# Turning the tokens of the first norm into columns: TensorE transposes replaced by VectorE block transposes and transfers through DRAM

## The chip, the cores and the metric

The kernel runs on one core of a Trainium2 chip. A core has TensorE (PE, matmuls; its weight loads are listed as PEld), VectorE (DVE), ScalarE (ACT), GpSimd (POOL) and SyncE (SP, which here only issues transfers). Each engine executes its own instructions in order. Data lies in SBUF (128 partitions), matmul results in PSUM, inputs and scratch in DRAM; transfers between DRAM and SBUF are issued on the queues of SP, ACT or POOL. The metric is the device time of one execution in microseconds, as the median of several runs.

## The reference, cut to what matters

One decoder layer on 1024 tokens of width 1024, in float32:

```python
z = h @ w_in                      # -> pooling group | q | k | v
mix = concat(pool_mixer(..), sliding_window_attention(..)) @ w_out
h = layer_norm(DEEPNORM_ALPHA * h + mix, ln1_g, ln1_b)     # the first norm
ff = square(relu(h @ w_ff1)) @ w_ff2                       # 1024 -> 4096 -> 1024
h = layer_norm(DEEPNORM_ALPHA * h + ff, ln2_g, ln2_b)
gate = sigmoid(h @ w_ple_gate + b_ple_gate)
h = h + gate * (p @ w_ple)
```

The first norm works on rows: a token lies on one partition and its 1024 features lie along it. `h @ w_ff1` needs the same numbers as columns: a feature on each partition and the tokens along it. Between the two the 1024 x 1024 matrix has to be transposed. This is what the change is about.

## The kernel before

**Tiles.** Tokens go in eight tiles `n` of 128. Every fp32 matrix is kept as a high part and a low part (`high`, L101, a cast on ACT; `low`, L106, a subtraction on DVE), and every product of two matrices is three matmuls (`mm3`, L116 to L118): high times high, high times low, low times high.

**Stages.** The layer runs in this order: input projection, attention and pooling (to about 208 us); the output projection, in which `out_left(0)`, `out_right(0..3)` finish tokens 0 to 511 and `out_left(1)`, `out_right(4..7)` finish tokens 512 to 1023; the first norm; the first half of the feed-forward; its second half; the second norm and the gate.

**The first norm.** `norm1(n)` (L544) does five things. `layer_norm` (L405) normalises the row tile `hn[n]` in place: two statistics and two full-width passes on DVE (L408, L424, L121), one pass on ACT (L423), one small power on POOL (L417). `transposed` (L444) then turns the tile on TensorE: eight transposes of 128 x 128 into two PSUM tiles, four into one of the two `pt` buffers (`tr_ps`), four into the single `av` buffer (`tr_av`). ACT scales the row tile and stores it to DRAM scratch `h_dram` for the second norm (L549, L550). Last, the columns are split from PSUM into high and low parts in SBUF (`split_to`, L538). For n below 4 these go to the operands `X["11"]` and `X["21"]`, and for n below 3 a plain copy of the first half goes to `pre`. For n of 4 and above the feed-forward's seven-product scheme (Strassen's kind) wants sums of blocks: `r12`, `t1`, `t2` are formed on ACT and DVE, and the splits go to `X["22"]`, `T1`, `T2` and `T3`. `last_sum` (L574) later forms `T4`.

**The feed-forward's first half.** `early(p)` (L598) for p = 0 to 7 multiplies weight block pairs with `X["11"]` and, in `rest`, with `X["21"]`: 24 matmuls per p in PSUM tiles `mm`. Then a list `order` of products with `T2`, `T3`, `T1`, `22`, `T4` follows, 12 matmuls each, in PSUM tiles `f`; each product's weights are split by `w_split` four products ahead (`AHEAD`).

**Where the order comes from.** The program text gives each instruction a place; the framework's planner then simulates a timeline from its own estimates of durations and writes a fixed order for each engine, taking an instruction of later text first if it is ready first. Buffers come from rings under a tag: `temp` (tag `t`, 6 buffers of 128 x 512), `part` (tag `ws`, 6 of 128 x 1024), `nat` (tag `n`, 8 of 128 x 1024), `wt` (tag `w`, 2). Waits for buffers and data are semaphores that the framework adds. In the text before, `norm1(0..3)` stand behind `out_left(1)`, and `norm1(4..7)` stand ahead of `early(1)`, `early(3)`, `early(5)` and `early(7)`.

**A turn without TensorE** exists already for the second norm: `flip` (L427). DVE transposes blocks of 32 x 32 of a whole 128 x 1024 tile (L429), one transfer stores the result to DRAM scratch `t_dram` (L430), and four transfers bring it back, each filling 32 partitions with pieces from all partitions (L432). All five transfers are on POOL's queue.

Of the kernel before, what the change touches and what calls it, by code (L numbers as in the profile page):

```python
# [61 lines left out]
NPRE = 8  # L62
NSUM = 3
PLAIN = 4
HALVES = (slice(0, HALF), slice(HALF, D))
NLAST = NPAIR - 4
AHEAD = 4
# [3 lines left out]
def layer(ctx, tc, xT, x, pT, w_in, w_pool, pscale, sinks, w_out, ln1, w1, w2, ln2, w_ple, w_gate, bgate, bias, rcount, out):  # L71
# [7 lines left out]
    def nm(s):  # L79
        uid[0] += 1  # L80
        return f"{s}_{uid[0]}"
# [23 lines left out]
    def low(eng, dst, src, hi):  # L105
        return eng.tensor_tensor(out=dst, in0=src, in1=hi.bitcast(F32), op=ALU.subtract)  # L106
# [67 lines left out]
    def tr_ps():  # L174
        return ps.tile([P, 4, P], F32, tag="pt", bufs=2, name=nm("pt"))
# [259 lines left out]
            )  # L435
        return t.rearrange("p (R k c) -> p R k c", R=4, k=NK)

    def tr_av():
        return ps.tile([P, 4, P], F32, tag="av", bufs=1, name=nm("av"))

    def transposed(y, j, pt):
        for k in range(4):
            kt = 4 * j + k
            nc.tensor.transpose(pt[:, k, :], y[:, kt * P : (kt + 1) * P], ident)  # L444
        return pt
# [86 lines left out]

    X = {}

    def block(name, i, c):
        return X[name][:, i, :, c * P : (c + 1) * P].bitcast(F32)

    def split_to(name, c, src, eng):  # L538
        cs = slice(c * P, (c + 1) * P)
        dh = X[name][:, 0, :, cs]  # L540
        high(dh, src)
        return low(eng, X[name][:, 1, :, cs], src, dh)

    def norm1(n):  # L544
        t, c = n // 4, n % 4
        layer_norm(hn[n], gb1)
        a = transposed(hn[n], 0, tr_ps())
        b = transposed(hn[n], 1, tr_av())
        nc.scalar.mul(out=hn[n], in_=hn[n], mul=ALPHA)  # L549
        nc.scalar.dma_start(out=h_dram[n], in_=hn[n])  # L550
        if t == 0:
            if c < 3:
                nc.scalar.copy(out=pre[:, 4 + c].rearrange("p (k t) -> p k t", k=4), in_=a)
            split_to("11", c, a, nc.vector)
            split_to("21", c, b, nc.vector)
        else:
            r12, t1, t2 = temp((P, 4, P)), temp((P, 4, P)), nat([P, 4, P])
            nc.scalar.copy(out=r12, in_=a)
            if c < 3:
                add(t1, a, pre[:, 4 + c].rearrange("p (k t) -> p k t", k=4), ALU.subtract)  # L560
# [594 lines left out]
```

## Time and profile before

| | |
|---|---|
| median of 3 runs | 984.06 us (984.02 to 984.25) |
| the profiled execution's own time | 984.01 us |
| its span in the trace | 982.2 us |
| TensorE busy | 973.8 us, 99% of the span |
| VectorE busy | 750.4 us, 76% |
| ScalarE busy | 470.6 us, 48% |
| GpSimd busy | 129.5 us, 13% |
| moved by transfers | 172.13 MB |

The span is what the trace covers; 1.8 us of the execution's time lie around it. Matmuls are pipelined, so a matmul of 0.39 us can follow another after 0.23 us, and "busy" counts the overlap once. A row of a timeline gives the start, the duration, the engine, the line, the operation and the tiles, and in brackets the idle time before it with what ended it.

### The profile page before, as it was taken

How to read it: one execution, taken by the hardware profiler on the slowest of the kernel's cores; microseconds unless marked ns; L12 is line 12 of the kernel's file. 1: busy time of each engine (PE TensorE's matmuls, PEld its weight loads, DVE VectorE, ACT ScalarE, POOL GpSimd, SP SyncE). 2: the span in 40 equal slices, each digit the busy share in tenths (PEclk: the TensorE clock that was granted, in tenths of full speed). 3: DMA queues.
4: the chain of work that ended last, by engine and by line, in shares of the span. 5: the costliest groups of instructions: out<-in, count | busy, mean ns of one | idle time of the engine just before them, and what ended most of it. 6: DMA issues, size and time to landing. Idle time of an engine off the chain costs nothing.

```text
span 982.2 us, 12301 instructions
## 1 busy us (share of the span) xinstructions
PE 973.8 (99%) x4474; PEld 809.3 (82%) x4474; DVE 750.4 (76%) x1188; ACT 470.6 (48%) x749; POOL 129.5 (13%) x185
## 2 busy tenths in 40 slices
PE   9999999999999999999999999999999999999998
PEld 7888887888888888888888888888888888878887
DVE  5798888895868876867547666888657699799895
ACT  5676666543475443434444344443434354554341
POOL 0013552020010000110000000100011111203210
PEclk9999999999999999999999999999999999999999
DMA  6512142623152544896264794675788866762741
GB/s 220 183 65 86 44 150 75 219 82 115 69 198 103 197 150 159 298 324 242 78 245 172 278 322 149 150 243 194 207 217 190 223 158 225 252 193 77 257 148 55
DMA packets 48188, 172.13 MB, mean 175 GB/s; under 512 B 6016, under 2 KB 7168, under 8 KB 45312
## 3 DMA queue, kind: packets, MB, share of 16 engines
q1 hardware_dynamic: 35584, 130.05, 38.6%
q0 software_dynamic: 10960, 36.71, 14.6%
q10 hardware_dynamic: 1584, 4.59, 1.2%
q8 instruction: 35, 0.57, 0.2%
q14 instruction: 25, 0.20, 0.1%
HBM read 138.82 MB, written 32.51 MB: 174 GB/s over the span
## 4 chain that ended last, share of the span: by engine, by line
PE 94%; DVE 2%; DMA 2%; issue 1%; ACT 1%; DVEq 0%
PE f L117 21%; PE f L118 21%; PE f L116 21%; PE mm L116 8%; PE mm L118 8%; PE mm L117 8%; DMA ws<-in_w_gate 2%; PE pt L322 1%; PE s L299 1%; PE s L298 1%; PE av L328 1%; PE av L327 1%; DVE w L106 0%; PE s L116 0%; ACT c L101 0%
## 5 line engine op out<-in xcount | busy, mean ns | idle before, releaser
L117 PE MATMUL f<-x,w 128*128 128x512 f32 x448 | 174.0, 389 | 0.4 <-DVE x L106 0.4
L118 PE MATMUL f<-x,w 128*128 128x512 f32 x448 | 173.9, 389 | 0.0
L116 PE MATMUL f<-c,ws 128*128 128x512 f32 (+1 forms) x420 | 162.5, 387 | 0.0
L117 PE MATMUL f<-c,ws 128*128 128x512 f32 (+1 forms) x420 | 162.5, 387 | 0.0
L118 PE MATMUL f<-c,ws 128*128 128x512 f32 (+1 forms) x420 | 161.3, 387 | 0.0
L116 PE MATMUL f<-x,w 128*128 128x512 f32 x448 | 147.1, 389 | 0.1
L101 ACT CAST w<-st 128x1024 fp32r<-128x1024 f32 (+2 forms) x66 | 65.6, 999 | 100.2 <-issue 57.9
L106 DVE TENSOR_TENSOR w<-st,w 128x1024 fp32r<-128x1024 f32 (+2 forms) x66 | 77.5, 1177 | 46.9 <-ACT w L101 46.8
L117 PEld LDWEIGHTS f<-x,w 128*128 128x128 f32 x448 | 84.1, 188 | 18.8 <-DVE x L106 1.1
L116 PEld LDWEIGHTS f<-x,w 128*128 128x128 f32 x448 | 84.0, 188 | 17.9 <-ACT x L101 0.5
L118 PEld LDWEIGHTS f<-x,w 128*128 128x128 f32 x448 | 84.1, 188 | 17.3
L118 PEld LDWEIGHTS f<-c,ws 128*128 128x128 f32 x420 | 78.9, 188 | 16.5 <-DVE ws L106 0.4
L117 PEld LDWEIGHTS f<-c,ws 128*128 128x128 f32 x420 | 78.9, 188 | 16.0
L116 PEld LDWEIGHTS f<-c,ws 128*128 128x128 f32 x420 | 78.9, 188 | 16.0
L106 DVE TENSOR_TENSOR x<-ws,x 128x1024 fp32r<-128x1024 f32 x54 | 65.8, 1219 | 1.5 <-ACT x L101 1.5
L101 ACT CAST ws<-w 128x512 fp32r<-128x512 f32 x60 | 36.9, 622 | 52.0 <-PE f L118 26.5
L106 DVE TENSOR_TENSOR ws<-w,ws 128x512 fp32r<-128x512 f32 x60 | 41.2, 690 | 25.3 <-ACT ws L101 24.6
L101 ACT CAST x<-ws 128x1024 fp32r<-128x1024 f32 x54 | 56.6, 1048 | 7.4 <-DMA ws<-gT 4.0
L101 ACT CAST ws<-st 128x512 fp32r<-128x512 f32 x48 | 29.8, 620 | 62.2 <-DVE st L121 30.8
L116 PE MATMUL mm<-c,w 128*128 128x512 f32 x144 | 56.4, 396 | 0.3 <-ACT w L101 0.3
L118 PE MATMUL mm<-c,w 128*128 128x512 f32 x144 | 56.6, 394 | 0.0
L117 PE MATMUL mm<-c,w 128*128 128x512 f32 x144 | 56.4, 393 | 0.0
(236 smaller groups left out, 1905.5 us busy)
## 6 DMA issues: line engine op xcount, KB each, us to landing
ws<-in_w SPq DMA_DIRECT2D x70, 512.0 KB, 3.8
w<-in_w SPq DMA_DIRECT2D x16, 1024.0 KB, 5.4
c<-fd SPq DMA_DIRECT2D x6, 2048.0 KB, 8.6
fd<-n POOLq DMA_DIRECT2D x20, 512.0 KB, 4.3
ws<-in_w POOLq DMA_DIRECT2D x20, 512.0 KB, 7.6
st<-in_w_in SPq DMA_DIRECT2D x17, 512.0 KB, 3.4
ws<-in_w_gate SPq DMA_DIRECT2D x16, 512.0 KB, 4.6
w<-in_w SPq DMA_DIRECT2D x10, 512.0 KB, 4.0
```

The source lines that it names most:

```text
L101: nc.scalar.copy(out=dst, in_=src)
L106: return eng.tensor_tensor(out=dst, in0=src, in1=hi.bitcast(F32), op=ALU.subtract)
L116: nc.tensor.matmul(o, ah, bh, start=first, stop=False, skip_group_check=more)
L117: nc.tensor.matmul(o, ah, bl, start=False, stop=False, skip_group_check=more)
L118: nc.tensor.matmul(o, al, bh, start=False, stop=last, skip_group_check=more)
L298: nc.tensor.matmul(s[:, i, dst], ql, kt[:, 0, g, kk : kk + kn], start=True, stop=False)
L299: nc.tensor.matmul(s[:, i, dst], ql, kt[:, 1, g, kk : kk + kn], start=False, stop=True)
L322: nc.tensor.transpose(pt[:, i, :], e[:, i, kb * P : (kb + 1) * P], ident)
L327: nc.tensor.matmul(av, VV[0][:, blk, g], pp[:, 0], start=(kb == lo), stop=False)
L328: nc.tensor.matmul(av, VV[0][:, blk, g], pp[:, 1], start=False, stop=(kb == 1))
```

## The change

`norm1` no longer uses TensorE. A new `flip_halves` transposes 32 x 32 blocks on DVE in two halves of 128 x 512, stores each half to DRAM scratch (`t_dram`, with a new shape) from SP's queue, and gathers the columns back with four transfers of 32 partitions each, two on SP's queue and two on POOL's. The turned tile lies in a `part` buffer for n below 4 and in a `nat` buffer above. The splits into high and low parts, with the sums, move into a function of their own, `spread(n)`, which reads the columns from SBUF. `norm1(0..3)` are each followed by their `spread`; `norm1(4)` and `norm1(5)` now stand behind `out_right(4)` and `out_right(5)`, `norm1(6)` and `norm1(7)` ahead of `early(1)` and `early(2)`, and `spread(4..7)` stand behind `rest()` in the steps p = 2, 3, 5 and 6.

```diff
+SPREAD = {2: 4, 3: 5, 5: 6, 6: 7}
...
-    t_dram = [tc.dram_tile([P, 4, 2 * P], F32, name=f"td{n}") for n in range(2 * NT)]
+    t_dram = [tc.dram_tile([4, 2, P, P] if n < NT else [P, 4, 2 * P], F32, name=f"td{n}") for n in range(2 * NT)]
...
-    def tr_av():
-        return ps.tile([P, 4, P], F32, tag="av", bufs=1, name=nm("av"))
...
+    def flip_halves(y, t, d):
+        for h in range(2):
+            b = temp()
+            nc.vector.transpose(
+                out=b.rearrange("p (q k c) -> p q k c", q=4, k=4),
+                in_=y[:, h * HALF : (h + 1) * HALF].rearrange("p (k q r) -> p q k r", k=4, q=4),
+            )
+            nc.sync.dma_start(out=d[:, h].rearrange("q p e -> p q e"), in_=b.rearrange("p (q e) -> p q e", q=4))
+        for q in range(4):
+            (nc.sync if q < 2 else nc.gpsimd).dma_start(
+                out=t[32 * q : 32 * q + 32].rearrange("r (m e) -> r m e", m=8),
+                in_=d[q].rearrange("h (R r) e -> r (h R) e", R=4),
+            )
+        return t.rearrange("p (h R k c) -> p h R k c", h=2, R=4, k=4)
...
     def norm1(n):
-        t, c = n // 4, n % 4
         layer_norm(hn[n], gb1)
-        a = transposed(hn[n], 0, tr_ps())
-        b = transposed(hn[n], 1, tr_av())
+        turned[n] = flip_halves(hn[n], nat([P, D]) if n > 3 else part((P, D), F32), t_dram[n])
         nc.scalar.mul(out=hn[n], in_=hn[n], mul=ALPHA)
         nc.scalar.dma_start(out=h_dram[n], in_=hn[n])
+
+    def spread(n):
+        t, c = n // 4, n % 4
+        ft = turned.pop(n)
+        a, b = ft[:, 0], ft[:, 1]
...
     for n in range(4):
         norm1(n)
+        spread(n)
     residual_left(1, os)
     for n in range(4, NT):
         out_right(n)
+        if n < 6:
+            norm1(n)
...
     for p in range(1, NPRE + 1):
-        if p % 2 and p // 2 < 4:
-            norm1(4 + p // 2)
+        if p < 3:
+            norm1(5 + p)
         after = early(p) if p < NPRE else None
         rest()
+        if p in SPREAD:
+            spread(SPREAD[p])
         rest = after
```

The views of `X` that `split_to`, `block` and `pre` use are regrouped to the order in which the columns lie in the turned tile; the numbers of elements and of instructions in the splits stay the same.

More of the change, by code (lines that the diff above doesn't have):

```diff
@@ L533, in layer, with columns, quarters @@
     X = {}
+    def columns(name, i, c):
+        return X[name][:, i, :, c * P : (c + 1) * P].rearrange("p k (R c) -> p R k c", R=4)
     def block(name, i, c):
-        return X[name][:, i, :, c * P : (c + 1) * P].bitcast(F32)
+        return columns(name, i, c).bitcast(F32)
     def split_to(name, c, src, eng):
-        cs = slice(c * P, (c + 1) * P)
-        dh = X[name][:, 0, :, cs]
+        dh = columns(name, 0, c)
         high(dh, src)
-        return low(eng, X[name][:, 1, :, cs], src, dh)
+        return low(eng, columns(name, 1, c), src, dh)
+    def quarters(t):
+        return t.rearrange("p (R k c) -> p R k c", R=4, k=4)
+    turned = {}
+    def flip_halves(y, t, d):
[12 more added lines that the diff above has]
+        return t.rearrange("p (h R k c) -> p h R k c", h=2, R=4, k=4)
     def norm1(n):
-        t, c = n // 4, n % 4
         layer_norm(hn[n], gb1)
-        a = transposed(hn[n], 0, tr_ps())
-        b = transposed(hn[n], 1, tr_av())
+        turned[n] = flip_halves(hn[n], nat([P, D]) if n > 3 else part((P, D), F32), t_dram[n])
         nc.scalar.mul(out=hn[n], in_=hn[n], mul=ALPHA)
         nc.scalar.dma_start(out=h_dram[n], in_=hn[n])
+    def spread(n):
+        t, c = n // 4, n % 4
+        ft = turned.pop(n)
+        a, b = ft[:, 0], ft[:, 1]
         if t == 0:
             if c < 3:
-                nc.scalar.copy(out=pre[:, 4 + c].rearrange("p (k t) -> p k t", k=4), in_=a)
+                nc.scalar.copy(out=quarters(pre[:, 4 + c]), in_=a)
             split_to("11", c, a, nc.vector)
@@ L556, in norm1 @@
         else:
-            r12, t1, t2 = temp((P, 4, P)), temp((P, 4, P)), nat([P, 4, P])
+            r12, t1, t2 = quarters(temp()), quarters(temp()), quarters(nat([P, HALF]))
             nc.scalar.copy(out=r12, in_=a)
             if c < 3:
-                add(t1, a, pre[:, 4 + c].rearrange("p (k t) -> p k t", k=4), ALU.subtract)
+                add(t1, a, quarters(pre[:, 4 + c]), ALU.subtract)
             else:
```

## The prediction

> **What bounds the kernel now.** I first read the page's busy shares and the chain of work that ended last.
>
> ```profile
> PE 973.8 (99%) x4474; PEld 809.3 (82%) x4474; DVE 750.4 (76%) x1188; ACT 470.6 (48%) x749; POOL 129.5 (13%) x185
> ...
> PEclk9999999999999999999999999999999999999999
> ...
> PE 94%; DVE 2%; DMA 2%; issue 1%; ACT 1%; DVEq 0%
> ```
>
> TensorE is busy for 973.8 of 982.2 us at the full granted clock, and 94% of the last chain is its own instructions. An instruction taken from TensorE shortens the kernel as long as everything that feeds it keeps up. The next view is the busy time by stretch, asked for the stretches around the first norm (columns: PE, PEld, DVE, ACT, POOL, clock, DMA share, GB/s).
>
> ```profile
> 226.00:234.00 8.00, 8.00 (x37) 6.63 (x36) 2.12 (x4) 0.00 (x0) 0.00 (x0) 1.00 0.21 70
> 286.00:296.00 10.00, 10.00 (x52) 8.35 (x51) 6.88 (x11) 8.15 (x15) 1.08 (x2) 1.00 0.67 239
> 306.00:316.00 10.00, 10.00 (x46) 8.28 (x45) 9.81 (x17) 5.56 (x10) 1.03 (x2) 1.00 0.13 52
> ```
>
> TensorE never stands still here. VectorE is the second engine: idle for 5.9 of 8 us while `out_left(1)` runs, but full from 306 to 316 us, right behind the stage that the change touches. So the question is twofold: how much TensorE time do the transposes hold, and does VectorE have the room, early enough, for what it is given?
>
> **What is removed.** The instructions by tile, and three rows of TensorE's timeline:
>
> ```profile
> L444 PE MATMUL pt<-ident,n x32: 270/272/273, 234.1 to 295.4; 128*128 128x128 f32 x32
> L444 PE MATMUL av<-ident,n x32: 270/272/273, 234.5 to 298.6; 128*128 128x128 f32 x32
> ...
> 212.32 0.39 PE L116 MATMUL mm<-w,c 128*128 128x512 f32 x1
> ...
> 234.08 0.60 PE L444 MATMUL pt<-ident,n 128*128 128x128 f32 x4
> ...
> 306.90 0.39 PE L116 MATMUL f<-c,ws 128*128 128x512 f32 x1
> ```
>
> The 0.27 us of a transpose overlaps its neighbours and is no price. I take the price from distances between starts. From 212.32 to 234.08 us stand the 96 matmuls of `out_left(1)` and nothing else: 21.76 / 96 = 0.2267 us a matmul. From 234.08 to 306.90 us stand all 64 transposes, the 96 matmuls of `out_right(4..7)` and the 192 of `early(0..7)`. Those 288 take 288 x 0.2267 = 65.28 us, so the transposes, with the slower matmuls just behind them, hold 72.82 - 65.28 = **7.54 us**, 0.118 us each. Half of them (n = 0 to 3) lie ahead of `early(0)`, the other half inside the early products: TensorE is 3.8 us ahead at `early(0)` (before: 306.9 - 192 x 0.2267 - 32 x 0.118 = 259.6 us) and 7.5 us ahead at 306.9 us.
>
> [...]
>
> **What is added on VectorE.** Two transposes of 128 x 512 per tile, 16 in all. The nearest row is `flip`'s of twice the width, in the second norm:
>
> ```profile
> L429 DVE STREAM_TRANSPOSE n<-n x4: 1232/1240/1248, 900.6 to 932.7; 128x1024 f32<-128x1024 f32 x4
> ```
>
> Half of 1.24 is 0.62 us; upper bound 1.24, if the time did not fall with the width; I take 0.62, since the other DVE operations of 512 and 1024 columns in this stage stand at 0.69 to 1.22. So 16 x 0.62 = 9.9 us (19.8 at the upper bound). The splits themselves stay: as many instructions, of SBUF instead of PSUM; "c<-pt" and "c<-n" rows below show the same price, so I cost this at nothing.
>
> ```profile
> L106 DVE TENSOR_TENSOR c<-n,c 128x512 fp32r<-128x512 f32 x4 | 2.7, 684 | 0.0
> L106 DVE TENSOR_TENSOR c<-pt,c 128x512 fp32r<-128x512 f32 x4 | 2.7, 680 | 0.7 <-ACT c L101 0.7
> ```
>
> **Does VectorE have room?** VectorE's and TensorE's timelines at the tightest place, the first products with sums:
>
> ```profile
> 216.24 1.22 DVE L121 TENSOR_TENSOR n<-n,st 128x1024 f32<-128x1024 f32 x1
> ...
> 218.63 1.29 DVE L106 TENSOR_TENSOR ws<-ws,ws 128x512 fp32r<-128x512 f32 x2
> ...
> 220.50 1.29 DVE L106 TENSOR_TENSOR ws<-ws,ws 128x512 fp32r<-128x512 f32 x2
> ...
> 223.92 1.29 DVE L106 TENSOR_TENSOR ws<-w,ws 128x512 fp32r<-128x512 f32 x2 [0.55 <-ACT ws L101]
> 225.13 1.22 DVE L121 TENSOR_TENSOR n<-n,st 128x1024 f32<-128x1024 f32 x1
> ...
> 269.31 1.22 DVE L121 TENSOR_TENSOR n<-n,st 128x1024 f32<-128x1024 f32 x1
> ...
> 313.42 0.69 DVE L106 TENSOR_TENSOR ws<-st,ws 128x512 fp32r<-128x512 f32 x1
> ...
> 317.62 0.69 DVE L106 TENSOR_TENSOR ws<-w,ws 128x512 fp32r<-128x512 f32 x1
> ...
> 317.79 0.39 PE L116 MATMUL f<-c,ws 128*128 128x512 f32 x1
> ...
> 226.00:246.00 20.00, 10.17 (x21) 1.00 0.21 80
> 246.00:306.00 60.00, 47.00 (x83) 1.00 0.38 141
> ```
>
> The L121 rows are the ends of the norms of n = 2 (217.5 us), n = 3 (226.4 us) and n = 7 (270.5 us). The fifth product with sums begins at 317.8 us, the sixth 12 matmuls later, 317.79 + 12 x 0.2267 = 320.5; their weight splits (L106) end at 314.1 and 318.3. The sixth has the least margin, 2.2 us. With TensorE 7.5 us early and VectorE given 9.9 us more, VectorE must fill 7.5 + 9.9 - 2.2 = **15.2 us** of what is idle before. The last two rows (VectorE alone) show 9.8 us idle from 226 to 246 and 13.0 us from 246 to 306: 22.8 us. Two thirds of it has to be used. I think it is, for three reasons from the rows. First, the idle 9.8 us lies exactly where the transposes and splits of n = 0 to 3 go: their norms end by 226.4 us, and their splits no longer wait for TensorE's transposes at 234. Second, part of the later idle time is waiting for those same transposes:
>
> ```profile
> ACT pre L553 <- PE pt L444: 13.6, 2, 10.3
> ACT n L549 <- PE av L444: 8.9, 2, 4.7
> DVE t L121 <- ACT t L558: 3.0, 2, 2.5
> ```
>
> Third, norm 7 ended at 270.5 us but its last four transposes came at 298.6 us, so its splits fell into 299 to 306 us, ahead of the full stretch; with columns from DRAM they can be done near 280 us. Against it: four of the six `ws` buffers now hold turned tiles, so that raw and split weights of `early(0)` and `early(1)`, split by 225 us before (the three L106 rows of two each), come after the first spreads: 3 x 1.29 = 3.9 us move behind 226 us. The six transposes of n = 0 to 2 (3.7 us) can take the places left free, as these norms have ended by 217.5 us: no net demand. Cover gone: each us of the 15.2 not found costs one us.
>
> **The transfers, on the path of the columns.** Per tile: two stores of 256 KB on SP, two gathers of 128 KB on SP and two on POOL, 64 in all, 16 x 0.25 + 32 x 0.125 = 8 MB. Nearest rows (size, median us to landing), and the extremes of the existing gathers and stores:
>
> ```profile
> hd<-n ACTq DMA_DIRECT2D x8, 512.0 KB, 2.6
> td<-n POOLq DMA_DIRECT2D x8, 512.0 KB, 3.6
> n<-td POOLq DMA_DIRECT2D x32, 128.0 KB, 5.5
> ...
> DMA to landing us min/median/max: 3.0/3.6/8.7
> ...
> DMA to landing us min/median/max: 2.7/5.5/7.9
> ```
>
> From the end of the norm to columns: 1.24 + 3.6 + 5.5 = 10.3 us, at most 1.24 + 8.7 + 7.9 = 17.8, with some issue time. n = 3: 226.4 + 17.8 = 244, spread by 247; `early(0)` wants it at 259.6 - 3.8 = 255.8. n = 7: 270.5 + 17.8 = 288 at worst, its spread (8 DVE operations, 5 us) 293; wanted at 306.9 - 7.5 = 299.4. Both hide, with 6 to 9 us left at the worst landing. The DMA share of 0.13 to 0.67 leaves room for 8 MB.
>
> **The queues that they join.** A gather waits for its stores on SP and on POOL. Behind it on SP stand weight loads, on POOL the next norm's power (L417) and the stores of `rest`. A wait of SP's queue, the last weight load of the early products with its landing and its first cast, and POOL's wait for the norms:
>
> ```profile
> SPq L600 <- DVE ws L106: 53.6, 4, 44.4
> ...
> L600 SPq DMA_DIRECT2D w<-in_w x1: 328/328/328, 282.1 to 282.1; - x1
> ...
> DMA to landing us min/median/max: 3.0/3.0/3.0
> ...
> 286.78 0.61 ACT L101 CAST ws<-w 128x512 fp32r<-128x512 f32 x1
> ...
> POOL sm L417 <- DVE sm L422: 68.6, 7, 23.7
> ```
>
> SP stands for 44 us in one wait for a weight buffer; loads are issued as soon as a buffer is free. The last, at 282.1 us, lands at 285.1 and is cast from 286.8, while its first product, `early(7)`'s, begins three products of 12 ahead of 306.9, at 306.9 - 36 x 0.2267 = 298.7 us. Its first split ends at 286.8 + 0.6 + 0.7 = 288.1, so 10.6 us cover a gather that waits 3.6 us for its store in front of such a load; the load itself moves up with TensorE, as its buffer comes free earlier. POOL waits up to 23.7 us for a norm's statistics; nothing there is close. ACT's store to `h_dram` now waits for DVE's transposes and comes earlier than behind TensorE's. I take zero, between 0 and 3.6 us (one store's wait, uncovered).
>
> **Sum.** 984.01 - 7.54 + 0 + 0 = **976.5 us** for the profiled execution; the median of the runs is 0.05 us above it, so the same figure is the forecast. After 306.9 us nothing depends on absolute time: TensorE stands still there for 0.4 us and for 82 - 78.1 = 3.9 us at the end.
>
> ```profile
> PE f L117 <- DVE x L106: 0.4, 1, 0.4
> ...
> 900.00:982.00 82.00, 78.11 (x373) 65.70 (x371) 66.24 (x98) 27.08 (x40) 11.12 (x20) 1.00 0.45 148
> ```
>
> **Rivals.** (1) VectorE absorbs only part: with u us of idle time used, the time is 976.5 + (15.2 - u). If all 9.8 us up to 246 and a quarter of the 13.0 behind are used, u = 13.1 and the time is 978.6; with 9.8 alone, 981.9. For it: the full stretch 306 to 316. Against: the three reasons above.
> (2) VectorE becomes the bound, and the kernel slower: its place is the sixth product with sums, its price 15.2 - u, and it decides when u is below 7.6. If the columns of n = 0 to 3 came so late that the 9.8 us went unused and half of the 13.0 us was found, u = 6.5 and the time 985.2; with nothing found 991.7. For it: transposes at 1.24 us would ask for 7.5 + 19.8 - 2.2 = 25.1 us of 22.8, and with the same 15.2 us found the time would be 986.4. Against: the landings above. [...]
> (3) The transfers come late: a wait on SP or POOL holds a weight load or the next tile's gathers. With the worst chain twice, n = 3 arrives at 226.4 + 35.6 = 262 us, is spread by 265, and costs 265 - 255.8 = 9 us: 985.7. Against: the idle queues.
> (4) The planner places the rest differently and a stall eats the gain: 984.
>
> **Chances.** Forecast 0.58 (975.5 to 978.0); rival (1) 0.19 (978 to 983.5); (2) 0.11; (3) 0.05; (4) 0.07. The range must leave out no more than 0.2: up to 984.0 it leaves out (2), (3) and half of (4); down to 975.2 it takes in the 0.4 us and 0.9 of the 3.9 us at the end, should other placing win them. A measurement of this kernel can tell about 0.2% (2 us) from no change. Faster: forecast and nearly all of (1), 0.76; the same: (4) and the end of (1), 0.09; slower: (2) and (3) with a little more, 0.15.
>
> **What would show it.** Right: no L444 rows; 288 matmuls between the end of `out_left(1)` and the first `f` in 65.3 us; 16 DVE transposes near 0.62 us; columns back within 18 us of the norm; no TensorE wait on L106 between 295 and 330 us. Wrong: a TensorE wait of microseconds on a split of `ws` or `c`, transposes near 1.2 us, or DMA landings over 9 us named before the splits.

## The result, and the profile after

The changed kernel takes 987.3 us (median of 15 runs, 985.33 to 992.4); the kernel before, run beside it, 984.23 us (15 runs, 982.81 to 986.08). The ratio is 1.0031 with a 95% interval of 1.002 to 1.0042: slower by 0.31%, about 3 us, where 7.5 us less were forecast. The profiled execution of the changed kernel is the slowest of its 15 (992.4 us, span 990.6), 5.1 us above the median, so its stalls show where time goes and not what the median execution loses at each place. Line numbers are those of each kernel: L117 after is L116 before, L107 is L106, L424 is L423, L455 is L457.

The page of the kernel after: busy time by engine, the shares of the chain that ended last, and the transfers' sum. The last row is the sum of the kernel before.

```profile
PE 971.1 (98%) x4410; PEld 802.0 (81%) x4410; DVE 757.6 (76%) x1204; ACT 471.2 (48%) x749; POOL 138.1 (14%) x201
...
PE 77%; DVE 9%; DMA 9%; issue 3%; ACT 1%; POOL 0%; SPq 0%; ACTq 0%; DVEq 0%; POOLq 0%
...
DMA packets 61757, 180.52 MB, mean 182 GB/s; under 512 B 6784, under 2 KB 20224, under 8 KB 58880
```
```profile
DMA packets 48188, 172.13 MB, mean 175 GB/s; under 512 B 6016, under 2 KB 7168, under 8 KB 45312
```

The 64 transposes are gone from TensorE (4474 to 4410 instructions) and VectorE has its 16 more (1188 to 1204). Both were meant. New is the chain: DMA has 9% of it and VectorE 9%, where each had 2%. The transfers add 8.4 MB in 13,569 packets, most of them of under 2 KB (20224 for 7168).

TensorE's timeline of the kernel after gives two marks: the first matmul of `early(0)` and the first product `f`.

```profile
255.96 0.39 PE L117 MATMUL mm<-c,ws 128*128 128x512 f32 x1
...
260.95 0.47 PE L117 MATMUL mm<-c,ws 128*128 128x512 f32 x1 [2.12 <-DVE n L455]
...
281.01 0.50 PE L117 MATMUL mm<-c,ws 128*128 128x512 f32 x1 [1.93 <-ACT t L617]
...
296.59 0.50 PE L117 MATMUL mm<-c,ws 128*128 128x512 f32 x1 [1.69 <-ACT pre L627]
...
310.37 0.73 PE L117 MATMUL f<-c,ws 128*128 128x512 f32 x2 [1.03 <-ACT c L102]
```

`early(0)` begins at 255.96 us, 3.6 us ahead of the 259.6 us worked out for the kernel before. The first `f` begins at 310.37 us, 3.5 us behind its 306.90. Between the marks stand 192 matmuls, 43.5 us at 0.2267 us each, and 54.4 us go by: **10.9 us are lost there**, and the waits in brackets are part of it. TensorE waits for a residual on VectorE that frees a PSUM tile (L455), for a relu (L617) and a copy (L627) on ACT that free one, and for a cast of columns (L102). None of these instructions is new. They are late.

Why late? First the windows around the stage, of the kernel before (226 to 234 and 286 to 296 us stand in the prediction) and then of the kernel after, with the same columns as there.

```profile
234.00:246.00 12.00, 12.00 (x67) 10.14 (x65) 8.06 (x18) 7.63 (x12) 0.55 (x1) 1.00 0.21 87
```
```profile
215.00:226.00 11.00, 11.00 (x50) 9.12 (x49) 10.76 (x19) 4.34 (x4) 2.55 (x4) 1.00 0.89 270
226.00:234.00 8.00, 8.00 (x37) 6.61 (x36) 2.86 (x6) 2.62 (x4) 0.59 (x1) 1.00 1.08 286
234.00:246.00 12.00, 12.00 (x55) 9.92 (x54) 7.07 (x14) 3.33 (x6) 2.82 (x5) 1.00 0.85 273
...
286.00:296.00 10.00, 8.91 (x40) 7.04 (x38) 7.69 (x13) 6.72 (x14) 2.40 (x5) 1.00 1.02 284
```

The last two columns are the share of time in which the DMA engines are busy and GB/s. The DMA engines, busy for 0.21 of the time from 226 to 246 us before, are full (shares near 1), and full again from 286 to 296, where they had 0.67. ACT and VectorE are *less* busy than before from 234 to 246 us (3.33 for 7.63 us, 7.07 for 8.06), though VectorE was given more. They are not short of time. They wait. The transfers between 205 and 310 us, before and after (size, median us from issue to landing):

```profile
w<-in_w SPq DMA_DIRECT2D x6, 512.0 KB, 4.0
```
```profile
td<-t SPq DMA_DIRECT2D x16, 256.0 KB, 4.6
...
w<-in_w SPq DMA_DIRECT2D x6, 512.0 KB, 7.2
...
ws<-td SPq DMA_DIRECT2D x8, 128.0 KB, 4.3
...
ws<-td POOLq DMA_DIRECT2D x8, 128.0 KB, 7.5
```

The store of a turned half takes 4.6 us, a gather of the first four tiles 4.3 on SP and 7.5 on POOL (the prediction had 3.6 for a store and 5.5 for a gather). Every group of transfers that was there before takes longer, by 1.4 to 2.5 times: a weight load 7.2 for 4.0 us, a row tile of x 10.5 for 4.9, a store of `rest` 3.7 for 2.6. Transfers on SP (the weight load), on POOL (the store of `rest`) and on ACT (the scaled rows, 5.8 for 2.6) alike are longer.

Now what stands in line behind the columns. Rows of the timelines of the kernel after: VectorE's transposes, then ACT, then three rows of SP's queue (stores of n = 2, gathers of n = 2 and 3, raw weights), and last norm 4's final instruction on VectorE:

```profile
215.14 2.49 DVE L552 STREAM_TRANSPOSE t<-n 128x512 f32<-128x512 f32 x4
...
221.11 1.30 DVE L552 STREAM_TRANSPOSE t<-n 128x512 f32<-128x512 f32 x2
...
230.85 0.62 ACT L576 COPY pre<-ws 128x512 f32<-128x512 f32 x1 [7.34 <-DMA ws<-td]
...
235.77 0.62 ACT L576 COPY pre<-ws 128x512 f32<-128x512 f32 x1 [2.30 <-DMA ws<-td]
...
243.50 0.62 ACT L576 COPY pre<-ws 128x512 f32<-128x512 f32 x1 [6.06 <-DMA ws<-td]
...
250.68 1.14 ACT L102 CAST ws<-ws 128x512 fp32r<-128x512 f32 x2 [5.52 <-DMA ws<-in_w]
...
251.73 1.15 ACT L424 ACTIVATE n<-n,sm 128x1024 f32<-128x1024 f32 x1
...
225.66 3.19 SPq L556 DMA_DIRECT2D td<-t  x2
...
238.06 4.80 SPq L558 DMA_DIRECT2D ws<-td  x4
242.91 0.97 SPq L623 DMA_DIRECT2D ws<-in_w  x2
...
257.13 1.22 DVE L122 TENSOR_TENSOR n<-n,st 128x1024 f32<-128x1024 f32 x1
```

The same two instructions of norm 4 in the kernel before, on ACT and on VectorE:

```profile
244.57 1.16 ACT L423 ACTIVATE n<-n,sm 128x1024 f32<-128x1024 f32 x1
```
```profile
247.46 1.23 DVE L121 TENSOR_TENSOR n<-n,st 128x1024 f32<-128x1024 f32 x1
```

The transposes of n = 0 end at 216.4 us, of n = 1 at 217.6 and of n = 2 at 222.4; their columns are used on ACT at 230.85, 235.77 and 243.50, that is 14.5, 18.1 and 21.1 us later, where the prediction had 9.1 and at worst 16.6 from there. The medians over the whole stage hide what the landings are in the crowd. The eight gathers of n = 0 and 1, issued from 218.88 to 229.24 us, land after 4.3 to 11.7 us, six of them after more than 8 us. For n = 2, SP issues the stores at 225.66 us, 3.3 us after the transposes; they land after 9.5 and 10.4 us, and only then, at 238.06, can the gathers be issued, which land after 4.3; the columns are used 5.4 us after that issue. ACT stands still for 7.34 + 2.30 + 6.06 us in front of these copies. Its next work is the cast of `early(0)`'s raw weights, which SP could issue only at 242.91 us, behind the gathers: 5.52 us more. Only then comes the centring of norm 4, at 251.73 us instead of 244.57, and norm 4 ends 9.7 us later than before. Its store and gathers, and those of norms 5 to 7, fall into 261 to 306 us, together with the scaled rows and the weight loads of the early products, and the same begins again.

### The profile page after: what moved, and what is told of

The parts are those of the page before. It is cut to its first block, busy times and chain, and to the rows that moved or that the text cites. A ratio compares the mean times of both kernels' runs of the same rounds, so it can differ in the third digit from the quotient of the medians.

```text
span 990.6 us, 12286 instructions
## 1 busy us (share of the span) xinstructions
PE 971.1 (98%) x4410; PEld 802.0 (81%) x4410; DVE 757.6 (76%) x1204; ACT 471.2 (48%) x749; POOL 138.1 (14%) x201
## 2 busy tenths in 40 slices
DMA packets 61757, 180.52 MB, mean 182 GB/s; under 512 B 6784, under 2 KB 20224, under 8 KB 58880
## 4 chain that ended last, share of the span: by engine, by line
PE 77%; DVE 9%; DMA 9%; issue 3%; ACT 1%; POOL 0%; SPq 0%; ACTq 0%; DVEq 0%; POOLq 0%
PE f L119 19%; PE f L118 19%; PE f L117 19%; PE mm L117 5%; PE mm L119 5%; PE mm L118 5%; DMA ws<-in_w_gate 2%; DMA ws<-in_w 2%; DVE x L107 2%; DMA td<-t 2%; DMA n<-td 1%; DVE w L107 1%; PE pt L323 1%; DMA ws<-td 1%; DMA ws<-gT 1%
## 5 line engine op out<-in xcount | busy, mean ns | idle before, releaser
L117 PE MATMUL f<-c,ws 128*128 128x512 f32 (+1 forms) x420 | 162.8, 388 | 1.0 <-ACT c L102 1.0
L117 PE MATMUL f<-x,w 128*128 128x512 f32 x448 | 147.2, 389 | 0.6 <-ACT x L102 0.6
L102 ACT CAST w<-st 128x1024 fp32r<-128x1024 f32 (+2 forms) x66 | 65.7, 998 | 101.0 <-issue 58.1
L107 DVE TENSOR_TENSOR w<-st,w 128x1024 fp32r<-128x1024 f32 (+2 forms) x66 | 77.4, 1176 | 46.0 <-ACT w L102 45.7
L117 PEld LDWEIGHTS f<-x,w 128*128 128x128 f32 x448 | 84.0, 188 | 18.4 <-ACT x L102 1.0
L117 PEld LDWEIGHTS f<-c,ws 128*128 128x128 f32 x420 | 78.8, 188 | 18.0 <-ACT c L102 1.5
L107 DVE TENSOR_TENSOR x<-ws,x 128x1024 fp32r<-128x1024 f32 x54 | 65.7, 1216 | 0.6 <-ACT x L102 0.6
L102 ACT CAST ws<-w 128x512 fp32r<-128x512 f32 x60 | 36.9, 621 | 59.2 <-PE f L119 29.7
L102 ACT CAST x<-ws 128x1024 fp32r<-128x1024 f32 x54 | 56.6, 1049 | 5.1 <-PE f L119 3.4
L107 DVE TENSOR_TENSOR ws<-w,ws 128x512 fp32r<-128x512 f32 x60 | 41.2, 687 | 23.4 <-ACT ws L102 22.8
L102 ACT CAST ws<-st 128x512 fp32r<-128x512 f32 x48 | 29.7, 620 | 58.2 <-DVE st L122 31.0
L117 PE MATMUL mm<-c,w 128*128 128x512 f32 x144 | 56.7, 398 | 0.1
```

What stands on the lines that cost most here:

```text
L102: nc.scalar.copy(out=dst, in_=src)
L117: nc.tensor.matmul(o, ah, bh, start=first, stop=False, skip_group_check=more)
```

## The experiments

Each ratio is to the kernel before on the same chip, with its 95% interval in brackets. Four theories were held against each other. **D**: VectorE has no room for its transposes. **W**: four of the six `ws` buffers are lent to turned tiles, and the weights wait for them. **C**: the transfers are too many and land late. **Q**: instructions that wait for columns stand in the queues ahead of work that mustn't wait. Theory T of the expectations is C and Q together. The mark to look at is the first `f`: 306.90 us before, 310.37 after, 299.4 by the forecast.

**No transfers.** The transposes write straight into the turned tile; the 16 stores and 32 gathers are gone.

```diff
-            b = temp()
             nc.vector.transpose(
-                out=b.rearrange("p (q k c) -> p q k c", q=4, k=4),
+                out=t[:, h * HALF : (h + 1) * HALF].rearrange("p (q k c) -> p q k c", q=4, k=4),
...
-            nc.sync.dma_start(out=d[:, h].rearrange("q p e -> p q e"), in_=b.rearrange("p (q e) -> p q e", q=4))
-        for q in range(4):
-            (nc.sync if q < 2 else nc.gpsimd).dma_start(
-                out=t[32 * q : 32 * q + 32].rearrange("r (m e) -> r m e", m=8),
-                in_=d[q].rearrange("h (R r) e -> r (h R) e", R=4),
-            )
```

> The changed kernel with VectorE's 16 transposes kept and all 48 transfers of the turn left out: VectorE writes its 32 x 32 blocks straight into the tile that the splits read, so the columns are not the reference's. Theory T (the transfers come late, and what waits for them stands in ACT's and VectorE's queues ahead of the norms): all 7.5 us come back, 976.5 us, between 975.5 and 979. Theory D (VectorE's 16 x 0.68 = 10.8 us more are too much for it): nothing comes back, 985 to 988. Theory W (the turned tiles of n = 0 to 3 hold four of the six ws buffers, so that the weights of the first early products come late): most comes back too, as the buffers come free sooner, 977 to 981.

Measured: 978.65 us, ratio 0.9941 (0.9928 to 0.9954). TensorE's first `f`, its wait on a weight split, and a window right behind that wait (PE busy, clock, DMA share, GB/s):

```profile
299.37 0.62 PE L117 MATMUL f<-c,ws 128*128 128x512 f32 x2
```
```profile
PE f L119 <- DVE ws L107: 2.6, 2, 2.0
```
```profile
436.30:439.70 3.40, 3.40 (x9) 0.50 0.85 267
```

The mark is at 299.37 us, where the forecast put it. So the price of the transposes on TensorE was right, VectorE does find the 15.2 us, and D falls: what costs the time is the transfers and what they bring along. W is not tested here: its range (977 to 981) holds the result too. The end is 6.2 us earlier in the median, not 7.5. In this profile TensorE waits 2.0 us for a split until 436.05 us and then runs at half the clock for 3.4 us, which costs some 1.7 us more. But this execution took 983.02 us, 4.4 above the median, and its granted clock is 0.997; the other four have 0.999 or 1.000 and so don't show that stretch. Why the median lacks 1.3 us of the 7.5 stays open.

**No transposes.** The transfers stay, VectorE's 16 transposes go.

```diff
-            b = temp()
-            nc.vector.transpose(
-                out=b.rearrange("p (q k c) -> p q k c", q=4, k=4),
-                in_=y[:, h * HALF : (h + 1) * HALF].rearrange("p (k q r) -> p q k r", k=4, q=4),
-            )
+            b = y[:, h * HALF : (h + 1) * HALF]
```

> The changed kernel with all 48 transfers kept and VectorE's 16 transposes left out: the stores read the row tile itself, so the columns are not the reference's. Theory T: the stalls stay, 984 to 988 us. Theory D: 976.5 to 979. Theory W: the stalls stay, 984 to 988.

Measured: 985.93 us, ratio 1.0013 (1.0004 to 1.0022). Without any work added on VectorE the kernel is still slower than before, by 1.1 us, and its first `f` comes at 306.73 us. The longest wait of TensorE and the window behind it:

```profile
PE mm L117 <- ACT t L613: 3.3, 1, 3.3
```
```profile
284.20:287.60 3.40, 3.40 (x9) 0.50 0.04 12
```

A stall at a relu is there as in the changed kernel (at 281 us), and longer (it ends at 283.21 us here).

**Turned tiles in `pre`.** The first four turned tiles go into `pre`, which is free at that time, so that no `ws` buffer is lent; the copy of a first half to `pre` (L576) falls away.

```diff
-        turned[n] = flip_halves(hn[n], nat([P, D]) if n > 3 else part((P, D), F32), t_dram[n])
+        turned[n] = flip_halves(hn[n], nat([P, D]) if n > 3 else pre[:, 2 * n : 2 * n + 2].rearrange("p h c -> p (h c)"), t_dram[n])
...
-            if c < 3:
-                nc.scalar.copy(out=quarters(pre[:, 4 + c]), in_=a)
```

> The changed kernel with the turned tiles of n = 0 to 3 gathered straight into pre, two slots each, in place of four ws buffers; three copies of 0.6 us on ACT go with it, and the weights of the first two early products can be loaded and split as early as before the change. Theory W: the wait of 5.5 us on ACT for the raw weights and with it most stalls go, 977 to 980 us. Theory T: ACT still waits for columns of n = 0 to 2 ahead of norm 4 and later for those of n = 4 to 7, 982 to 986. Theory D: 984 to 988.

Measured: 987.46 us, ratio 1.0028 (1.0018 to 1.0038). The buffers made no difference that shows, and W falls as the cause of the loss: the raw weights are issued at 207.99 and 215.75 us here, and norm 4's centring on ACT still begins only at 249.39 us. The time is above the ranges of W and T; it lies in that of D, which the run without transfers has ruled out. A wait for a residual, at another place than in the changed kernel, is the longest here:

```profile
PE mm L117 <- DVE n L455: 4.7, 1, 4.7
```

**One half of the tiles each.** Tiles 4 to 7 alone by transfers, with 0 to 3 on TensorE as before; and the reverse, with the text order of norms 4 to 7 as before.

```diff
+        if n in (0, 1, 2, 3):        # the other kernel: (4, 5, 6, 7)
+            av = ps.tile([P, 4, P], F32, tag="av", bufs=1, name=nm("av"))
+            turned[n] = [transposed(hn[n], j, pt).rearrange("p k (R c) -> p R k c", R=4) for j, pt in ((0, tr_ps()), (1, av))]
+        else:
             turned[n] = flip_halves(hn[n], nat([P, D]) if n > 3 else part((P, D), F32), t_dram[n])
```

> The turn by VectorE and transfers for n = 4 to 7 alone; n = 0 to 3 are transposed on TensorE and spread as before the change. 32 transposes come back, 32 x 0.118 = 3.8 us of TensorE. Theories T and W, if the harm begins with the first four tiles: norm 4 is on time again and the time is 984.1 - 3.8 = 980.3 us, between 979.5 and 982. If the late columns of the last four alone are enough: 983 to 986. Theory D: half of the added work, 984 to 986.

> The turn by VectorE and transfers for n = 0 to 3 alone; n = 4 to 7 are transposed on TensorE and spread as before the change, ahead of the odd early products. Theory T, if a late norm 4 is what costs: ACT waits for columns of n = 1 and 2 and for raw weights ahead of norm 4 as in the changed kernel, norms 4 to 7 come 9 us late, and TensorE's transposes wait for them: 983 to 986 us. Theory L (only the columns of the last four, needed inside the early products, are too late): 984.8 - 3.8 = 981.0, between 980 and 982.

Measured: the last four 986.46 us, ratio 1.0019 (1.0007 to 1.0031); the first four 984.43 us, ratio 0.9992 (0.9984 to 1.0001). Neither half brings its 3.8 us, and the last four lose by themselves, half a us above the range given for late columns of the last four alone. So lateness has a place of its own behind 266 us, not only the one that n = 0 to 3 hand on: with the last four, TensorE waits 1.8 us for the copy to `pre` at 302 us. The first four fell into the range of a late norm 4 (983 to 986), but not by that mechanism. Norm 4's centring is late there, at 250.08 us, and yet no wait of TensorE in the early products is over 0.3 us. At the first `f` both kernels are ahead of the kernel before, by 2.7 us (first four, 304.23) and 2.0 (last four, 304.92). What turns this into no gain and into a loss lies behind that mark, outside the stage that was changed, and no run isolates it.

**Held consumers, first try.** If Q is right, the consumers of columns belong behind the work that mustn't wait. On the kernel with turned tiles in `pre`, the spreads of n = 2 and 3 are held behind norm 4, those of n = 4 to 7 behind the copy and the weight split of their product; 0 and 1 stay where they were.

```diff
+            with tc.issue_after(done[0].ins), tc.issue_after(done[1].ins):   # norm 4
+                spread(2)
+                spread(3)
...
+            with tc.issue_after(copies[-1].ins), tc.issue_after(lows[-1].ins):
                 spread(SPREAD[p])
```

> The kernel with the turned tiles in pre (all 48 transfers kept), and the places of the spreads in the queues changed by hand: those of n = 2 and 3 stand behind norm 4 on ACT and VectorE, those of n = 4 to 7 behind the copy to pre and the weight splits of the early product of their step. Theory Q (late columns cost only through what stands behind them in ACT's and VectorE's queues): most stalls go, 978 to 981 us. Theory C (the transfers themselves crowd the weight loads and the copies out): 983 to 988.

Measured: 997.87 us, ratio 1.0129 (1.0116 to 1.0142): a clear miss, worse than every other kernel. Its waits of TensorE:

```profile
PE f L117 <- ACT ws L102: 4.1, 1, 4.1
PE mm L117 <- DVE n L455: 4.0, 1, 4.0
```

The wait for the residuals is still there, as 0 and 1 were not held, and a new one of 4.1 us for a weight cast has come, far behind the stage, at 440 us. The run did not say whether holding is wrong or held the wrong ones.

**Fewer, larger transfers.** The transposes go into the turned tile itself, four stores of 128 KB in pieces of 1 KB on SP and POOL, and one gather of 512 KB on SP: 5 transfers a tile for 6, in larger pieces. A second kernel adds the holds of the first try.

```diff
+                out=t.rearrange("p (q k c) -> p q k c", q=4, k=NK)[:, :, 4 * h : 4 * h + 4],
...
+        for R in range(4):
+            (nc.sync if R < 2 else nc.gpsimd).dma_start(
+                out=d.rearrange("(q r) R e -> r q R e", q=4)[:, :, R],
+                in_=t[32 * R : 32 * R + 32].rearrange("r (q e) -> r q e", q=4))
+        nc.sync.dma_start(out=t, in_=d.rearrange("p R e -> p (R e)"))
```

> The changed kernel with another cut of the transfers: VectorE transposes into the turned tile itself, four stores per tile (one for each 32 partitions, pieces of 1 KB) and one gather of 512 KB (4 KB a partition) bring the columns back into it. The same 8.4 MB, 40 transfers instead of 48, and 8192 + 1024 pieces instead of 16384. Theory C (pieces of 512 bytes keep the 16 engines busy): columns land sooner and half or more of the 9 us of stalls goes, 978 to 983 us. Theory Q: as the planner's places stay about the same, 983 to 987.

> Both: the transfers in place and the spreads held behind norm 4 and behind the early products' own copies and splits. Theories C and Q, if both act: 977 to 980 us. If neither is the cause: 984 to 988.

Measured: 989.03 us, ratio 1.0041 (1.0029 to 1.0053), and with the holds 988.74 us, ratio 1.0031 (1.0019 to 1.0043). Both lie above their ranges, and neither is an improvement on the changed kernel. Rows of VectorE's timeline and TensorE's longest wait in the first:

```profile
236.67 1.29 DVE L107 TENSOR_TENSOR c<-ws,c 128x512 fp32r<-128x512 f32 x2 [10.39 <-ACT c L102]
237.88 1.28 DVE L455 SCALAR_TENSOR_TENSOR n<-n,mm 128x512 f32<-128x512 f32 x2
```
```profile
PE mm L117 <- DVE n L455: 4.9, 1, 4.9
```

The first row is the place to look at. VectorE stands for 10.39 us in front of the split of n = 0's columns, and the residuals of `out_left(1)` (L455), whose last matmul starts at 233.35 us, are behind it; TensorE waits for the PSUM that they would free. With the holds of the first try this wait is 5.2 us long. C is not ruled out by this: the crowd did not become thinner (a weight load lands after 6.8 us, a row tile of x after 10.2), so the run says only that transfers cut this way do not help by themselves. That pieces of 512 bytes keep the DMA engines busy, as the expectation has it for C, is not shown: in larger pieces their share of busy time from 226 to 246 us is 0.86 (0.85 from 234 to 246 us in the changed kernel). And the place that the holds had left out has a name: the spreads of n = 0 and 1, ahead of the residuals.

**All consumers held.** The spreads of n = 0 and 1 go behind the last residual of `out_left(1)`; the rest as in the kernel just above.

```diff
-        spread(n)
-    residual_left(1, os)
+    left = residual_left(1, os)
+    with tc.issue_after(left.ins):
+        spread(0)
+        spread(1)
```

> The transfers in place with all eight spreads held back: those of n = 0 and 1 stand behind the four residuals of the left half on VectorE, those of n = 2 and 3 behind norm 4, those of n = 4 to 7 as in the run with both. Theory Q (columns late by some 10 us cost through the residuals, norms and copies queued behind them, and through the half clock that a stall of over 2 us brings): the stall of 5.2 us before a residual between 226 and 246 us goes, with its 3.4 us or less of half clock, and the time falls from 988.7 to 980 to 983. Theory C (crowded transfers delay the weight loads and rows themselves): no fall below 985.

Measured: 981.16 us, ratio 0.9958 (0.9944 to 0.9972): faster than both kernels, with all eight tiles turned by transfers. TensorE's first `f`, its longest wait near this stage, and the landing of the weight loads:

```profile
300.62 0.62 PE L117 MATMUL f<-c,ws 128*128 128x512 f32 x2
```
```profile
PE f L118 <- DVE c L107: 1.0, 1, 1.0
```
```profile
w<-in_w SPq DMA_DIRECT2D x6, 512.0 KB, 7.5
```

The landings are no shorter than in the changed kernel (a weight load 7.5 us). Against the held kernel just above, only the places of the spreads of n = 0 and 1 differ, and the ratio falls from 1.0031 to 0.9958, 7 us. Against the changed kernel the cut of the transfers differs too; the next run leaves that out.

**The order alone.** The changed kernel with its own 48 transfers, and the three holds. The rest of the edit only hands the held-behind instructions on; the planner then orders the whole anew.

```diff
-        spread(n)
-    residual_left(1, os)
+    left = residual_left(1, os)
+    with tc.issue_after(left.ins):
+        spread(0)
+        spread(1)
...
+        if n == 4:
+            with tc.issue_after(done[0].ins), tc.issue_after(done[1].ins):
+                spread(2)
+                spread(3)
...
+            with tc.issue_after(copies[-1].ins), tc.issue_after(lows[-1].ins):
                 spread(SPREAD[p])
```

> The changed kernel's own 48 transfers with the same held places of all eight spreads as in the run that beat the kernel before (981.2 us with transfers in place). If the places in the queues alone turned the loss into the gain: 980.5 to 983 us. If the transfers in place were needed as well, because two gathers on POOL that wait for their stores hold the next norm's power there: 984 to 989.

Measured: 982.44 us, ratio 0.998 (0.9972 to 0.9989). From +0.31% to -0.2%, 5 us, by the places in the queues alone. The same rows as for the changed kernel: copies of columns and norm 4's centring on ACT with the mark on TensorE, then landings:

```profile
229.45 0.62 ACT L578 COPY pre<-ws 128x512 f32<-128x512 f32 x1 [6.49 <-DMA ws<-td]
234.18 0.62 ACT L578 COPY pre<-ws 128x512 f32<-128x512 f32 x1 [2.10 <-DMA ws<-td]
241.64 1.15 ACT L424 ACTIVATE n<-n,sm 128x1024 f32<-128x1024 f32 x1 [5.79 <-DVE sm L423]
242.70 0.60 ACT L578 COPY pre<-ws 128x512 f32<-128x512 f32 x1
...
301.06 0.73 PE L117 MATMUL f<-c,ws 128*128 128x512 f32 x2
```
```profile
w<-in_w SPq DMA_DIRECT2D x6, 512.0 KB, 7.1
ws<-td POOLq DMA_DIRECT2D x8, 128.0 KB, 7.5
```

The columns of n = 0, 1 and 2 are used at 229.45, 234.18 and 242.70 us, within 1.6 us of the changed kernel's times, and the landings are the same 7.1 and 7.5 us. What differs is norm 4's centring, 10.1 us earlier at 241.64, ahead of n = 2's columns. The mark is 9.3 us earlier between the two profiled executions; the medians differ by 4.9. So the crowd is the condition, and the order decides a large part of what it costs.

**Nobody waits for the columns.** The counterpart: as many transfers, but the gathers go into a second DRAM scratch, and VectorE transposes into the turned tile, from which the stores and the splits read.

```diff
+        back = tc.dram_tile([P, D], F32, name=nm("back"))
...
-                out=t[32 * q : 32 * q + 32].rearrange("r (m e) -> r m e", m=8),
+                out=back[32 * q : 32 * q + 32].rearrange("r (m e) -> r m e", m=8),
```

> The changed kernel with as many transfers of the same sizes, but nothing waits for them: the splits read VectorE's blocks directly, and the gathers write into a second scratch in DRAM. The columns are not the reference's. Theory Q (waiting for the columns is what costs): close to the run without transfers, 978 to 981 us. Theory C (the transfers crowd the weight loads, the rows of x and the stores, whoever waits for them): 983 to 987.

Measured: 985.76 us, ratio 1.0011 (1.0001 to 1.0022). With no consumer of columns on ACT or VectorE the kernel is no faster than before: none of the 7.5 us comes back. SP's queue, ACT and TensorE at the stall:

```profile
284.51 1.19 SPq L558 DMA_DIRECT2D back<-td  x2
285.79 0.55 SPq L623 DMA_DIRECT2D w<-in_w  x1
...
291.39 0.62 ACT L102 CAST ws<-w 128x512 fp32r<-128x512 f32 x1 [5.68 <-DMA w<-in_w]
...
293.06 0.50 PE L117 MATMUL mm<-c,ws 128*128 128x512 f32 x1 [3.62 <-ACT pre L627]
```

A weight load stands on SP behind two gathers that wait 8.0 us for their store, is issued at 285.79 us, and lands 5.6 us later; its cast holds ACT for 5.68 us, and the copy behind the cast (L627) keeps TensorE standing for 3.62. Behind it the clock is 0.50 from 293.55 to 296.90 us, another 1.7 us; the two are 5.3 of the 6.4 us by which the first `f` is later than without transfers (305.72 against 299.37). Q in its narrow form (only those who read columns wait) isn't enough: the gathers themselves are waiting instructions, on SP, ahead of loads. In these rows the load's issue, at 285.79 us, follows the gathers' (284.51 us, 1.19 long) within 0.1 us.

**Only some of the tiles, held.** Transfers in place with all holds for n = 0 to 3, or for n = 0 to 5, the other tiles on TensorE. The scaled rows of n = 0 to 3 (or of 2 and 3) are stored after the spreads instead of before.

```diff
+        if n < 4:                       # the other kernel: 6
             turned[n] = flip_halves(hn[n], part((P, D), F32), t_dram[n])
...
+                for i in range(4):      # the other kernel: (2, 3)
+                    keep_rows(i)
```

> The turn by transfers (in place) for n = 0 to 3 alone, spreads held behind the left residuals and norm 4, and the stores of the scaled rows of n = 0 to 3 put behind the spreads; n = 4 to 7 turned on TensorE. Theory Q: 985.2 - 3.8 = 981.4, between 980.5 and 983. Theory C: the crowd of stores, gathers, rows of x and weights from 215 to 246 us still costs, 983.5 to 986.

> Transfers in place for n = 0 to 5, spreads held; n = 6 and 7 turned on TensorE. 48 of 64 transposes come back: 984.6 - 48 x 0.118 = 979.0 us if the columns of n = 4 and 5 come in time (978 to 980.5). If the second burst of transfers still delays weight loads: 980.5 to 983, no better than the first four alone (981.0).

Measured: 981.01 us, ratio 0.9966 (0.9954 to 0.9979), and 980.41 us, ratio 0.9963 (0.9948 to 0.9978). With eight tiles the ratio was 0.9958; the three can't be told apart. Against the first four without holds (0.9992), holds, transfers in place, later stores and the norms 4 to 7, which stand behind `out_right` here and in the early products there, together bring 2.6 us (0.0026 x 984). Each of these kernels beats the kernel before and the changed kernel.

## Why the prediction was wrong, by its steps

- **What bounds the kernel**: right. TensorE's time is what counts, and without the transfers the end moves by 6.2 us in the median.
- **What is removed, 7.54 us**: right. 3.6 of 3.8 us ahead at `early(0)` in the changed kernel; 306.90 - 299.37 = 7.53 us ahead at the first `f` without transfers.
- **VectorE's transposes at 0.62 us**: right. Four in a row take 2.49 us, 0.62 each.
- **Does VectorE have room**: right about the work. The run without transfers reaches the mark with all 16 transposes on VectorE, and the run without transposes is still slower than before. So the amount of VectorE's work is not what costs, and rivals (1) and (2) are not the cause. But the condition that rival (2) named, columns so late that the idle 9.8 us go unused, did come: from 226 to 246 us VectorE works 2.86 + 7.07 = 9.9 of 20 us, no more than the 10.17 before. Its 985.2 us is near the result by luck, as it was worked out for another place, the sixth product with sums.
- **The transfers: this step failed.** It added the landings of existing transfers, called the worst chain 17.8 us, and found room in a share of 0.13 to 0.67. With the change the DMA engines are full (0.85 to 1.08 from 215 to 246 us), and from the end of the transposes to the use of the columns pass 14.5 to 21.1 us, where 9.1 and at worst 16.6 were taken. The mis-sized terms are the landings in the crowd: n = 2's stores take 9.5 and 10.4 us, where 3.6 and at worst 8.7 were taken, and the gathers of n = 0 and 1 up to 11.7, where 5.5 and at worst 7.9 were. (The number of transfers is a slip as well: 16 stores and 32 gathers are 48 and not 64; the 8 MB are right.) It also asked only when n = 3 and n = 7 are *wanted by TensorE*. It did not ask who stands behind n = 0, 1 and 2 on ACT: norm 4, on which all later columns hang.
- **The queues, cost zero: this step failed too.** The bound of 3.6 us was one store's wait in front of one load, with 10.6 us of cover. In the changed kernel the raw weights are issued at 242.91 us behind the gathers, and ACT waits 5.52 us for them. In the run in which nobody waits for columns one weight load behind two gathers costs TensorE 3.62 us.
- **VectorE's and ACT's places**: the step on VectorE's room priced the work and not its place. The 10.39 us in front of n = 0's split, with the residuals behind it, is the plainest case.
- **"Each us not found costs one us"**: not always. Some stalls were followed by a stretch at half the clock (next section but one), so they cost more than themselves: the 2.0 us wait without transfers some 1.7 us more. The prediction had no term for this.
- **"After 306.9 us nothing depends on absolute time"**: too strong. Without transfers 7.5 us at the mark are 6.2 at the end; with all spreads held, 306.90 - 300.62 = 6.3 us are 3.4 (ends by the medians). What lies behind the mark is shown below the list.
- **Rival (3)** had the mechanism, a wait that holds the next gathers or a weight load, and 985.7 us; measured are 987.3. That the number is near is luck, as it put the delay at `early(0)`, which in the run begins 3.6 us early. Its chance of 0.05 rested on "the idle queues". It named SP and POOL, and left out ACT and VectorE.

The windows from the first `f` to near the last matmul, of the kernel before and of the changed kernel (PE busy, clock, DMA share, GB/s):

```profile
306.90:978.00 671.10, 670.61 (x2983) 1.00 0.63 198
```
```profile
310.37:986.40 676.03, 672.83 (x2982) 1.00 0.63 196
```

TensorE is idle there for 0.5 and for 3.2 us (length less busy time), without transfers for 3.9 (2.0 of them the one wait for a split), with all spreads held for 3.1: mostly many waits of about 1 us or less. So some of the gain is lost behind the stage, with or without transfers, and what makes it so is open.

Open is how the loss divides between late landings and places in the queues for each tile: the order alone gives 5 us back, transfers in place about two more (0.998 to 0.9958, intervals that just touch), and the run without any transfer another 1.7 (0.9941, intervals that overlap). Even the two held kernels with all eight tiles gain only 2.0 and 4.1 of the 7.5 us (by their ratios). The first try at holding has its size from three stalls of 4.0, 3.5 and 4.1 us, each with a stretch at a lower clock (0.69 and 0.63 from 235 to 240 and from 240 to 245 us, 0.79 from 310 to 318, below 0.9 in the page's slice from 424 to 449). The clock of its profiled execution is 0.991 over the span of 997.6 us, so by estimate up to (1 - 0.991) x 997.6 = 9 us are lost by it; why the stalls came is open. And in the profiled execution of the changed kernel, 5.1 us above its median, 3.5 us of the added span are there at the first `f` and 4.9 come behind it; the experiments were not aimed at the latter.

## What to carry to other kernels

Price a new round trip through DRAM at the landing under the crowd that it makes, with all that the change moves into the same stretch, and not at the median of a quiet one. Then list for each instruction that will wait for the landing, the gathers on their queue too, what stands behind it on its engine (as the residuals behind VectorE's 10.39 us), and put it behind the work that mustn't wait: here the same 48 transfers cost 0.31% in the planner's order and gain 0.2% in a held one. The planner did not find this order by itself here. Nor does every hold help: the first try, which left n = 0 and 1 where they were, cost 1.29%.

## What the runs showed of the hardware that was not expected

After some stalls TensorE goes on at a granted clock of 0.50, half of full speed: in the run in which nobody waits for columns its matmuls start 0.43 us apart from 293.74 to 296.30 us, and 0.23 us apart again from 297.05 on. Behind the 2.0 us wait in the kernel without transfers the clock is 0.50 from 436.30 to 439.70 us, so (1 - 0.50) x 3.4 = 1.7 us of matmul time are lost on top of the wait; behind the 3.3 us wait in the kernel without transposes it is 0.50 for 3.4 us again (284.20 to 287.60). In the kernel with fewer transfers the 4.9 us stall is followed by twice that (PE busy, clock, DMA share, GB/s):

```profile
237.95:244.70 6.75, 6.09 (x14) 0.50 0.54 203
```

At half the clock over 6.09 us of work, 3.0 us go on top of 4.9. The stalls of 1.7 to 2.1 us in the changed kernel's profile (260.95, 281.01, 296.59 us) left its clock at 1.00 (from 260.90 to 264.40, 280.90 to 284.40 and 296.60 to 300.00 us), and in the kernel with fewer transfers, which has a wait of 2.2 us for the copy to `pre` (L627) as well, the clock is 1.00 in every window from 246 to 330 us. So not every stall of this size is followed by it, and no run shows the threshold that one expectation has, "a stall of over 2 us": a wait of 2.0 us was followed by half the clock, one of 2.12 us was not. What decides it is not shown.

The profile of the changed kernel hides that the clock is part of the loss. Over the whole span the granted clock was 0.996 to 0.998 in 12 of the changed kernel's 15 executions, and 1.000 in the profiled one; the kernel before has 0.999 or 1.000 wherever it ran beside the experiments, and the held order 1.000 in 9 of its 12. A clock lower by 0.001 to 0.002 over 985 us is an estimated 1 to 2 us, of a loss of 3.
